# One buffer for each channel tile of the activations, and buffers of its own for folding the norm gains into weights

## The chip, the cores and the metric

The kernel runs on one core of a Trainium2 chip, alone. The metric is the device time of one execution in microseconds. One execution of the kernel was recorded by the hardware profiler; times inside it are counted from its first instruction. PE is the engine of the matmuls, DVE, ACT and POOL are the other compute engines, and SP issues most of the transfers.

## The reference

A trunk of two layers on 2048 positions of 1024 channels, in float32: a gated short convolution, then stick-breaking attention with 8 heads of 64, whose keys and values are projected once.

```python
def _rmsnorm(x, g):
    return x * rsqrt(mean(x * x, axis=-1) + 1e-6) * g

def _short_conv_mixer(h, w_in, w_conv, w_out):
    b_gate, c_gate, xin, g = split(h @ w_in, 4)            # w_in: 1024 x 4096
    y = b_gate * causal_depthwise_conv3(c_gate * xin, w_conv)
    return (y * silu(g)) @ w_out

def _stick_breaking_attention(q, k, v):                    # for each block of 128 queries
    z = q @ k.T * scale
    log_one_minus = where(mask, log_sigmoid(-z), 0)        # mask: strictly causal
    weights = exp(where(mask, z + reverse_cumsum(log_one_minus), -inf))
    return weights @ v

x = x + _short_conv_mixer(_rmsnorm(x, norm_a), w_in_a, conv_a, w_out_a)
k, v = split(_rmsnorm(x, norm_kv) @ w_kv, 2)
q, g = split(_rmsnorm(x, norm_b) @ w_in_b, 2)
x = x + (_stick_breaking_attention(q, k, v) * silu(g)) @ w_out_b
out = _rmsnorm(x, norm_f)
```

## The kernel before

The activations are held transposed, channels on the 128 partitions (eight tiles of 128 channels, k = 0 to 7) and positions along the row, in four chunks c of 512 positions. Every large product is made of three matmuls for each k, on values split into a high and a low part: high weight with high activation, high with low, low with high (`mm3`, line 210). So one product of 128 output channels for one chunk is 24 matmuls of 128x128 by 512 columns. Splitting is a copy on ACT that rounds to the high part and a subtraction that leaves the low part, on DVE or POOL (`split`, line 172).

**Weights.** The first use of a block of weights (1024 x 128) loads it raw (`load_raw`, two buffers `wraw`), splits it into a `whl` tile (`w_tile`, four buffers, 8 KB for each partition) and stores that to memory (`split_w`). Later uses load the stored split (`load_w`). `fold_gains` does the same ahead of time for the 16 blocks of `w_kv` and `w_in_b`: it loads a block raw, multiplies it by the norm's gains on DVE (line 366), splits and stores it. It uses the same two `wraw` and four `whl` buffers as the mixer's weights.

**Activations.** `act_tile` gives a buffer for all eight channel tiles of a chunk, high and low (32 KB for each partition), and there are two of them. In turn they hold h (the normed input), y (the gated convolution, read back), xn (the normed stream after layer 0) and the gated attention output og. A third buffer of 16 KB, `og`, holds x1 (the stream after layer 0, eight tiles) and once og and x2. A buffer is handed to its next tile when everything that reads or writes the old tile is done, transfers included.

**Order of work.** `m01` makes the mixer input products for chunks 0 and 1 together, in eight blocks of columns `cb`. In a block the four weights C, X, B and G are used by chunk 0 and then by chunk 1 (192 matmuls). Beside it run the statistics of chunks 2 and 3 (`stats_x`) and `fold_gains`. Then come the output projection of the mixer and the K, Q, V and gate projections of each chunk, with mixer products of chunks 2 and 3 and the attention of earlier chunks between them. Chunk 3's attention and the last projections end the program. The program is written as such interleaved streams, and a scheduler then fixes the order of the instructions of each engine; each engine and SP's queue run theirs strictly in that order.

Of the kernel before, what the change touches and what calls it, by code (L numbers as in the profile page):

```python
# [14 lines left out]
P = 128  # L15
# [6 lines left out]
NR, NW, NT, NL, NWB, NRAW, NWTS = 5, 8, 4, 5, 4, 2, 2  # L22
# [23 lines left out]
def kernel(  # L46
# [68 lines left out]
    def act_tile(nm):  # L115
        return sb.tile([P, 2, KD, CH], F32R, name=nm, tag="act", bufs=2)
# [59 lines left out]
    def load_raw(src, nm, kt=KD):  # L176
        raw = sb.tile([P, kt, P], F32, name=f"wr_{nm}", tag="wraw", bufs=NRAW)
        if len(src.shape) == 2:
            src = src.rearrange("(k p) n -> p k n", p=P)
        nc.sync.dma_start(out=raw, in_=src)  # L180
        return raw

# [6 lines left out]
    def split_w(raw, key, nm, kt=KD, eng=nc.vector):  # L189

        wt = w_tile(nm, kt)
        split(wt[:, 0], wt[:, 1], raw, eng)
        split_d[key] = dram.tile([P, 2, kt, P], F32, name=f"sw_{nm}")
        nc.sync.dma_start(out=split_d[key], in_=wt.bitcast(F32))
        return wt

    def load_w(src, key, nm, kt=KD, eng=nc.vector):

        if key not in split_d:
            return split_w(load_raw(src, nm, kt), key, nm, kt, eng)  # L200
        wt = w_tile(nm, kt)
        nc.sync.dma_start(out=wt.bitcast(F32), in_=split_d[key])
        return wt
# [6 lines left out]
    def mm3(ps, wts, a, kt=KD):  # L210
# [3 lines left out]
        for k in range(kt):  # L214
            for w, m in ((hi, 0), (hi, 1), (lo, 0)):
                ins = nc.tensor.matmul(ps, w[:, k, :], a[:, m, k, :], start=n == 0, stop=n == 3 * kt - 1)  # L216
# [16 lines left out]
    def norm_x_late(c, between=None):  # L233

        hc = act_tile(f"h_{c}")
        xs = []
        for k in range(KD):
            if k == 1 and between is not None:
# [36 lines left out]
    def norm_x(c):  # L275
        hc = act_tile(f"h_{c}")
        pb = bcast(rx[c], f"hb{c}")
        for k in range(KD):
# [3 lines left out]
            split(hc[:, 0, k, :], hc[:, 1, k, :], x)  # L282
# [78 lines left out]
    def fold_gains():  # L361

        for nm, src, gain in (("kv", w_kv, gains["kv"]), ("b", w_in_b[0], gains["b"])):
            for i in range(KD):
                raw = load_raw(src[:, i * P:(i + 1) * P], f"fold_{nm}{i}")
                nc.vector.tensor_mul(raw, raw, gain.unsqueeze(2).to_broadcast([P, KD, P]))
                split_w(raw, (nm, i), f"{nm}{i}")
# [398 lines left out]
```

## Time and profile before

| | us |
|---|---|
| three runs: median (lowest to highest) | 1909.34 (1906.65 to 1910.77) |
| the profiled execution | 1907.57 |
| its span, first to last instruction | 1905.8 |
| PE busy | 1784.0 (94%) |
| DVE busy | 1264.6 (66%) |
| ACT busy | 769.7 (40%) |
| POOL busy | 436.2 (23%) |
| data moved | 443.64 MB, mean 233 GB/s |

Names in the profile are the program's tile names with buffer numbers left out: `whl_G` is the split weight G of the mixer, `whl_kv` and `whl_b` are folded blocks, `sw_...` is the stored split in memory, `wr_...` is a raw block, `pC`, `pX`, `pB` and `pG` are the mixer products, `po`, `pk`, `pq`, `pv` and `pg` the later projections, and `cs`, `p`, `cv` and `sg` the mixer's intermediate values. L216 is the matmul line of all large products, L173 and L174 are the two halves of every split, and L366 is the fold's multiplication. "SPq" is SP issuing a transfer. A number in brackets with an arrow is the idle time before an instruction and who ended it.

### The profile page before, as it was taken

The page shows a single profiled execution, that of the slowest core. Times are in us where ns is not written, and L with a number is a line of the kernel's source. Part 1 is how long each engine was busy: PE and PEld are TensorE (multiplying, and loading weights), DVE is VectorE, ACT ScalarE, POOL GpSimd, SP SyncE. Part 2 cuts the span into 40 slices and gives each one's busy share as a digit, 9 for nine tenths or more (in the row PEclk, how much of TensorE's full clock was granted, in tenths as well). Part 3 has the DMA queues.
Part 4 walks back from the last instruction along what each step waited for, and adds up shares of the span by engine and source line. Part 5 has one row for each costly group of instructions (what it writes and reads, how often), then busy time and mean ns, then how long its engine had stood idle before and what let it go on. Part 6 is the DMA issues. An engine that isn't in the chain of part 4 may idle for free.

```text
span 1905.8 us, 24702 instructions
## 1 busy us (share of the span) xinstructions
PE 1784.0 (94%) x8312; PEld 1449.4 (76%) x8312; DVE 1264.6 (66%) x1895; ACT 769.7 (40%) x1481; POOL 436.2 (23%) x822
## 2 busy tenths in 40 slices
PE   7899999999999999999999999999979999878785
PEld 5787777778888888888788888888857788656563
DVE  7644554574334264428888346788897999999996
ACT  6312222241123133314545233444555666565553
POOL 5000000000011021103123112222422224654641
PEclk9999999999999999999999999999999999999897
DMA  9648787798887779776767776655746665877751
GB/s 314 210 150 248 248 254 237 243 312 304 295 284 270 258 237 286 246 262 224 242 211 268 238 253 219 202 175 197 258 144 196 197 199 193 284 225 250 252 177 50
DMA packets 226702, 443.64 MB, mean 233 GB/s; under 512 B 16912, under 2 KB 131600, under 8 KB 199952
## 3 DMA queue, kind: packets, MB, share of 16 engines
q1 hardware_dynamic: 166496, 383.30, 60.0%
q10 hardware_dynamic: 59920, 58.74, 10.9%
q8 instruction: 66, 1.08, 0.2%
q14 instruction: 60, 0.49, 0.1%
q0 software_dynamic: 160, 0.02, 0.1%
HBM read 314.34 MB, written 127.66 MB: 232 GB/s over the span
## 4 chain that ended last, share of the span: by engine, by line
PE 69%; DVE 14%; DMA 9%; issue 4%; ACT 2%; POOL 1%; SPq 0%; ACTq 0%; POOLq 0%; DVEq 0%
PE pX L216 8%; PE po L216 7%; PE pG L216 7%; PE pC L216 7%; PE pB L216 6%; PE pg L216 5%; PE pk L216 5%; PE pq L216 5%; PE pv L216 4%; PE wt L512 4%; DVE R L500 4%; PE av L522 3%; DVE w L504 2%; PE av L521 2%; PE z L486 2%
## 5 line engine op out<-in xcount | busy, mean ns | idle before, releaser
L500 DVE TENSOR_TENSOR_SCAN R<-R,R,ones 128x512 f32<-128x512 f32 x192 | 256.6, 1339 | 11.4 <-ACT R L489 11.1
L489 ACT ACTIVATE R<-z 128x512 f32<-128x512 f32 (+1 forms) x320 | 174.2, 544 | 173.1 <-DVE R L500 78.4
L174 DVE TENSOR_TENSOR wtl<-wt,wth 128x512 fp32r<-128x512 f32 (+1 forms) x320 | 185.6, 600 | 67.2 <-ACT wth L173 66.3
L504 DVE TENSOR_TENSOR w<-w,R 128x512 f32<-128x512 f32 (+1 forms) x320 | 212.2, 671 | 21.3 <-POOL R L499 3.0
L173 ACT CAST wth<-wt 128x512 fp32r<-128x512 f32 (+1 forms) x320 | 160.3, 526 | 160.1 <-PE wt L512 137.4
L216 PE MATMUL pC<-h,whl_C 128*128 128x512 f32 x768 | 197.1, 405 | 14.4 <-ACT whl_C L173 8.3
L216 PE MATMUL pG<-h,whl_G 128*128 128x512 f32 x768 | 186.6, 393 | 9.9 <-ACT whl_G L173 9.9
L499 POOL COPY R<-R 128x1 f32<-128x1 f32 x192 | 112.3, 585 | 360.8 <-DVE R L500 293.3
L216 PE MATMUL pX<-h,whl_X 128*128 128x512 f32 x768 | 187.6, 393 | 6.0 <-ACT cs L320 3.9
L216 PE MATMUL po<-y,whl_o 128*128 128x512 f32 x768 | 187.8, 394 | 2.0 <-DVE x L389 1.3
L512 PE MATMUL wt<-ident,w 128*128 128x128 f32 x1088 | 177.8, 278 | 9.2 <-DVE w L504 5.1
L216 PEld LDWEIGHTS pC<-h,whl_C 128*128 128x128 f32 x768 | 148.2, 195 | 49.4 <-ACT whl_C L173 8.3
L216 PE MATMUL pB<-h,whl_B 128*128 128x512 f32 x768 | 185.6, 392 | 0.0
L216 PEld LDWEIGHTS pG<-h,whl_G 128*128 128x128 f32 x768 | 143.2, 188 | 41.0 <-ACT whl_G L173 11.6
L491 ACT ACTIVATE w<-z 128x512 f32<-128x512 f32 (+1 forms) x320 | 172.7, 543 | 0.5 <-PE wt L512 0.5
L216 PEld LDWEIGHTS pX<-h,whl_X 128*128 128x128 f32 x768 | 142.2, 188 | 37.6 <-ACT cs L320 5.1
L216 PEld LDWEIGHTS po<-y,whl_o 128*128 128x128 f32 x768 | 144.2, 189 | 33.5 <-DVE x L389 1.9
L512 PEld LDWEIGHTS wt<-ident,w 128*128 128x128 f32 x1088 | 138.6, 143 | 38.3 <-DVE w L504 7.2
L216 PEld LDWEIGHTS pB<-h,whl_B 128*128 128x128 f32 x768 | 143.0, 188 | 30.1 <-DVE cv L356 0.4
L522 PE MATMUL av<-wtl,vv 128*128 128x512 f32 (+1 forms) x320 | 129.1, 405 | 36.7 <-DVE wtl L174 36.6
L500 DVE TENSOR_TENSOR_SCAN R<-R,ones 128x512 f32<-128x512 f32 (+3 forms) x128 | 116.1, 913 | 33.8 <-POOL R L495 32.2
L486 PE MATMUL z<-kt,q 128*128 128x512 f32 (+1 forms) x320 | 129.1, 405 | 4.1 <-ACT w L491 3.4
(170 smaller groups left out, 2655.3 us busy)
## 6 DMA issues: line engine op xcount, KB each, us to landing
whl_o<-sw_o SPq DMA_DIRECT2D x24, 1024.0 KB, 5.7
kt<-k_d ACTq DMA_DIRECT2D x80, 256.0 KB, 3.6
vv<-v_d ACTq DMA_DIRECT2D x80, 256.0 KB, 4.0
whl_C<-sw_C SPq DMA_DIRECT2D x16, 1024.0 KB, 5.4
whl_X<-sw_X SPq DMA_DIRECT2D x16, 1024.0 KB, 5.5
whl_B<-sw_B SPq DMA_DIRECT2D x16, 1024.0 KB, 5.5
whl_G<-sw_G SPq DMA_DIRECT2D x16, 1024.0 KB, 5.2
whl_k<-sw_kv SPq DMA_DIRECT2D x16, 1024.0 KB, 5.2
```

Of the source, the lines that this page charges most:

```text
L173: nc.scalar.copy(hi, src)
L174: eng.tensor_sub(lo, src, hi.bitcast(F32))
L216: ins = nc.tensor.matmul(ps, w[:, k, :], a[:, m, k, :], start=n == 0, stop=n == 3 * kt - 1)
L486: nc.tensor.matmul(ps[:, lom:CH], q2[:, 0, qi * P:(qi + 1) * P], kt[:, lom:CH], start=True, stop=False)
L489: nc.scalar.activation(R[:, lo + 1:CH + 1], ps[:, lo:CH], AF.Sigmoid, scale=-0.125)
L491: nc.scalar.activation(w[:, lo:CH], ps[:, lo:CH], AF.Sigmoid, scale=0.125)
L499: nc.gpsimd.tensor_copy(R[:, 0:1], carry[qi])
L500: nc.vector.tensor_tensor_scan(out=R[:, lo + 1:CH + 1], data0=R[:, lo + 1:CH + 1], data1=ones[:, 0:1].to_broadcast([P, CH - lo]), initial= ...
L504: nc.vector.tensor_mul(w[:, lo:CH], w[:, lo:CH], R[:, lo:CH])
L512: nc.tensor.transpose(wt[:, qi * P:(qi + 1) * P], ws[qi][:, kb * P:(kb + 1) * P], ident)
L521: nc.tensor.matmul(av[:, 0:n], vs, wh[:, 0:n], start=first, stop=False)
L522: ins = nc.tensor.matmul(av[:, 0:n], vs, wl[:, 0:n], start=False, stop=final)
```

## The change

The two large activation buffers become 16 buffers of one channel tile each (high and low, 4 KB for each partition), taken one by one: `h`, `y`, `xn` and `og` are now lists of eight or four tiles, and a tile's buffer comes free when that tile's own readers are done. The 16 KB buffer `og` becomes eight buffers of 2 KB, which x1 and x2 take one channel tile at a time. og no longer sits in it, but in `act` tiles.

`fold_gains` no longer takes `wraw` and `whl` buffers. It works on half blocks (four of the eight k): two tiles from the eight `og` buffers, one for the high part and one for the low. The raw half block is loaded into the low tile, multiplied there, and split, and each part is stored by a transfer of its own. One folded block was one load of 512 KB and one store of 1024 KB; it is now two loads and four stores of 256 KB each. Nothing is computed differently.

```diff
-NR, NW, NT, NL, NWB, NRAW, NWTS = 5, 8, 4, 5, 4, 2, 2
+NR, NW, NT, NL, NWB, NRAW, NA, NWTS = 5, 8, 4, 5, 4, 2, 16, 2
...
-    def act_tile(nm):
-        return sb.tile([P, 2, KD, CH], F32R, name=nm, tag="act", bufs=2)
+    def act_tile(nm, k):
+        return sb.tile([P, 2, CH], F32R, name=f"{nm}_{k}", tag="act", bufs=NA)
...
             for i in range(KD):
-                raw = load_raw(src[:, i * P:(i + 1) * P], f"fold_{nm}{i}")
-                nc.vector.tensor_mul(raw, raw, gain.unsqueeze(2).to_broadcast([P, KD, P]))
-                split_w(raw, (nm, i), f"{nm}{i}")
+                split_d[nm, i] = dram.tile([P, 2, KD, P], F32, name=f"sw_{nm}{i}")
+                for j in range(0, KD, 4):
+                    hi, lo = (sb.tile([P, 4, P], F32R, name=f"fold{m}_{nm}{i}_{j}", tag="og", bufs=KD) for m in range(2))
+                    raw = lo.bitcast(F32)
+                    nc.sync.dma_start(out=raw, in_=src[j * P:(j + 4) * P, i * P:(i + 1) * P].rearrange("(k p) n -> p k n", p=P))
+                    nc.vector.tensor_mul(raw, raw, gain[:, j:j + 4].unsqueeze(2).to_broadcast([P, 4, P]))
+                    split(hi, lo, raw)
+                    for m, t in enumerate((hi, lo)):
+                        nc.sync.dma_start(out=split_d[nm, i][:, m, j:j + 4, :], in_=t.bitcast(F32))
                 yield 1.0
...
-        y = act_tile(f"y_{c}")
+        y = []
         for k in range(KD):
+            y.append(act_tile(f"y_{c}", k))
             t = ld512(f"yr_{c}_{k}")
             nc.sync.dma_start(out=t, in_=y_d[c][k])
-            split(y[:, 0, k, :], y[:, 1, k, :], t, nc.gpsimd if k in YLP else nc.vector)
+            split(y[k][:, 0, :], y[k][:, 1, :], t, nc.gpsimd if k in YLP else nc.vector)
...
-            if ob == 0:
-                x1 = sb.tile([P, KD, CH], F32, name=f"x1_{c}", tag="og", bufs=1)
-            x = x1[:, ob, :]
+            x = sb.tile([P, CH], F32, name=f"x1_{c}_{ob}", tag="og", bufs=KD)
+            x1.append(x)
...
-        if c not in og_t:
-            og_tile(c)
-        og = og_t[c]
+        og = act_tile(f"og_{c}", k)
+        og_t.setdefault(c, []).append(og)
```

The scheduler then puts the instructions in another order at some places. The first is SP's queue in the mixer stage. Its rows before, around the first folds, which stand behind the weights of the third block of columns (`y_d_2_89` is the store of chunk 0's y of that block):

```order
L194 DMA sw_B_0_1096<-whl_B_0_1093 128x2048
L180 DMA wr_fold_kv_1283<-in_w_kv_dram 128x8x128
L194 DMA sw_G_0_1192<-whl_G_0_1189 128x2048
L180 DMA wr_C_0_1353<-in_w_in_a_dram 128x8x128
L357 DMA y_d_1_96<-cv_1_924 128x512
L357 DMA y_d_2_89<-cv_0_1123 128x512
L377 DMA yr_2_2812<-y_d_2_89 128x512
L194 DMA sw_kv_1289<-whl_kv_1286 128x2048
L180 DMA wr_fold_kv_1387<-in_w_kv_dram 128x8x128
L194 DMA sw_C_0_1358<-whl_C_0_1355 128x2048
```

And now, in that third block, ahead of the same y store; the first fold load stands 63 rows further up, among the loads of the start:

```order
L191 DMA sw_C_0_980<-whl_C_0_975 128x2048
L188 DMA wr_B_0_1106<-in_w_in_a_dram 128x8x128
L367 DMA sw_kv_1727<-fold_kv_4_1737 128x512
L363 DMA fold_kv_4_1828<-in_w_kv_dram 128x4x128
L367 DMA sw_kv_1818<-fold_kv_0_1819 128x512
L367 DMA sw_kv_1818<-fold_kv_0_1820 128x512
L191 DMA sw_X_0_1073<-whl_X_0_1068 128x2048
L188 DMA wr_G_0_1202<-in_w_in_a_dram 128x8x128
L363 DMA fold_kv_0_1933<-in_w_kv_dram 128x4x128
L367 DMA sw_kv_1818<-fold_kv_4_1827 128x512
```

The folds have moved ahead: 13 of the 32 half blocks have been asked for at the end of these rows, where before one block of 16 was ahead of that y store, and the last store of a folded half stands before the y of the fifth block. From the y store of chunk 0's second block to that of its third, SP has nine fold loads, 18 fold stores, four raw weights, four spills of split weights and three y transfers. The eight loads of x1 for chunk 0, which stood at the start ahead of raw G, now stand behind the folds.

The second place is ACT at the end of the mixer stage, where the first y is split. Before (`y_2803` is the one tile of chunk 0's y):

```order
L173 CAST whl_G_0_2639<-wr_G_0_2637 128x1024
L173 CAST y_2803<-yr_0_2804 128x512
L173 CAST y_2803<-yr_1_2808 128x512
L173 CAST y_2803<-yr_2_2812 128x512
L173 CAST y_2803<-yr_3_2816 128x512
L320 COPY cs_1_2701<-pC_1_2676 128x512
L173 CAST whl_b_2736<-wr_fold_b_2733 128x1024
L173 CAST y_2803<-yr_4_2820 128x512
L351 ACTIVATE sg_0_2669<-sg_0_2669 128x512
```

And now:

```order
L334 ACTIVATE cv_0_2764<-p_0_2727,cw 128x512
L174 CAST y_0_2961<-yr_0_2962 128x512
L174 CAST y_1_2966<-yr_1_2967 128x512
L174 CAST y_2_2971<-yr_2_2972 128x512
L174 CAST y_3_2976<-yr_3_2977 128x512
L174 CAST y_4_2981<-yr_4_2982 128x512
L174 CAST y_5_2986<-yr_5_2987 128x512
L174 CAST y_6_2991<-yr_6_2992 128x512
L345 ACTIVATE sg_0_2818<-sg_0_2818 128x512
L314 COPY cs_1_2850<-pC_1_2825 128x512
```

Seven splits of y stand in a row ahead of `sg` and `cs`, each on a tile of its own, and no folded block stands between. On PE, the G product of chunk 0, which before was broken up after two matmuls in four of the eight blocks with the other chunk's C product put between, is now whole in these four.

The third place is DVE in the first block, between the inverse norms of chunk 0 and their use. Before:

```order
L155 TENSOR_SCALAR dg_h_1_422<-ident,yl_h_417 128x128 x4
L170 TENSOR_TENSOR acc_h_995<-acc_h_995,sq_h_1001 128x512
L174 TENSOR_TENSOR whl_G_0_442<-wr_G_0_440,whl_G_0_442 128x1024
L333 TENSOR_TENSOR p_0_377<-p_0_377,rs_0_430 128x512
L341 SCALAR_TENSOR_TENSOR cv_0_435<-p_0_377,cw,cv_0_435 128x512
```

And now:

```order
L156 TENSOR_SCALAR dg_h_1_429<-ident,yl_h_419 128x128 x4
L171 TENSOR_TENSOR acc_h_1009<-acc_h_1009,sq_h_1015 128x512
L175 TENSOR_TENSOR whl_G_0_447<-wr_G_0_448,whl_G_0_447 128x1024
L175 TENSOR_TENSOR whl_C_0_709<-wr_C_0_710,whl_C_0_709 128x1024
L364 TENSOR_TENSOR fold_kv_4_1307<-fold_kv_4_1307,g_kv 128x512
L171 TENSOR_TENSOR acc_h_1009<-acc_h_1009,sq_h_1020 128x512
L327 TENSOR_TENSOR p_0_384<-p_0_384,rs_0_437 128x512
```

A split of C and a fold's multiplication stand ahead of `p` here, and the two operations of the first fold stand further up; the third fold follows before the norms of chunk 1 are used. Between the first multiplication by chunk 1's norms and the multiplication of its convolution by B stood three sums of squares of this kind (`acc_h`), and now stands one.

More of the change, by code (lines that the diff above doesn't have):

```diff
@@ L174, in split @@
         eng.tensor_sub(lo, src, hi.bitcast(F32))
[L176 to L181, printed above, removed]
     def w_tile(nm, kt=KD):
@@ L187 @@
     split_d = {}
[L189 to L195, printed above, removed]
     def load_w(src, key, nm, kt=KD, eng=nc.vector):
         if key not in split_d:
-            return split_w(load_raw(src, nm, kt), key, nm, kt, eng)
+            wt = w_tile(nm, kt)
+            raw = sb.tile([P, kt, P], F32, name=f"wr_{nm}", tag="wraw", bufs=NRAW)
+            nc.sync.dma_start(out=raw, in_=src.rearrange("(k p) n -> p k n", p=P))
+            split(wt[:, 0], wt[:, 1], raw, eng)
+            split_d[key] = dram.tile([P, 2, kt, P], F32, name=f"sw_{nm}")
+            nc.sync.dma_start(out=split_d[key], in_=wt.bitcast(F32))
+            return wt
         wt = w_tile(nm, kt)
@@ L215, in mm3 @@
             for w, m in ((hi, 0), (hi, 1), (lo, 0)):
-                ins = nc.tensor.matmul(ps, w[:, k, :], a[:, m, k, :], start=n == 0, stop=n == 3 * kt - 1)
+                ins = nc.tensor.matmul(ps, w[:, k, :], a[k][:, m, :], start=n == 0, stop=n == 3 * kt - 1)
                 if fine[1] and len(anchors) > SLACK and n % GRP == 0:
@@ L281, in norm_x @@
                                            op0=ALU.mult, op1=ALU.mult)
-            split(hc[:, 0, k, :], hc[:, 1, k, :], x)
+            hc.append(act_tile(f"h_{c}", k))
+            split(hc[k][:, 0, :], hc[k][:, 1, :], x)
         return hc
@@ L392, in proj_out @@
             yield rest(24)
-        xn = act_tile(f"xn_{c}")
+        kept[c] = []
         pb = rstd_bcast(acc, f"x1{c}")
         for k in range(KD):
-            t = x1[:, k, :]
-            nc.vector.tensor_mul(t, t, pb)
-            split(xn[:, 0, k, :], xn[:, 1, k, :], t, nc.gpsimd if k in XNL else nc.vector)
-        kept[c] = xn
+            xn = act_tile(f"xn_{c}", k)
+            nc.vector.tensor_mul(x1[k], x1[k], pb)
+            split(xn[:, 0, :], xn[:, 1, :], x1[k], nc.gpsimd if k in XNL else nc.vector)
+            kept[c].append(xn)
         yield YP[c] * 24 * MM
@@ L568, in gated @@
             nc.gpsimd.tensor_mul(r, r, sg)
-        split(og[:, 0, k, :], og[:, 1, k, :], r)
+        split(og[:, 0, :], og[:, 1, :], r)
     def gated_in(c, ks=range(4)):
@@ L621, in out_b_last @@
     def out_b_last(c):
-        og, x2 = og_t[c], x2_t[0]
+        og = og_t[c]
+        x2 = [sb.tile([P, CH], F32, name=f"x2_{c}_{k}", tag="og", bufs=KD) for k in range(KD)]
         for ob in range(KD):
@@ L628, in out_b_last @@
             yield from mm3(ps, wts, og, kt=3)
-            nc.sync.dma_start(out=x2[:, ob, :], in_=x1_d[c][ob])
-            nc.vector.tensor_add(x2[:, ob, :], x2[:, ob, :], ps)
+            nc.sync.dma_start(out=x2[ob], in_=x1_d[c][ob])
+            nc.vector.tensor_add(x2[ob], x2[ob], ps)
             yield rest(9)
@@ L658, in out_b_last @@
             if k in (1, 4, 7):
[L659 to L660 removed]
+                nc.scalar.activation(x2[k], x2[k], AF.Copy, scale=gains["f"][:, k:k + 1])
+                nc.gpsimd.tensor_mul(x2[k], x2[k], pbs)
             else:
[L662 removed]
+                nc.vector.scalar_tensor_tensor(out=x2[k], in0=x2[k], scalar=gains["f"][:, k:k + 1],
                                                in1=pb, op0=ALU.mult, op1=ALU.mult)
[L664 removed]
+            nc.sync.dma_start(out=outT[k * P:(k + 1) * P, cols(c)], in_=x2[k])
         yield 0.0
```

35 lines of the change are left out of this document (11 added, 24 removed).

## The prediction

> **What bounds the kernel now.** I read the page first, then the stretches of the whole span, then PE's waits inside the stretch that has room, then the timeline around one such wait.
>
> ```profile
> span 1905.8 us, 24702 instructions
> PE 1784.0 (94%) x8312; PEld 1449.4 (76%) x8312; DVE 1264.6 (66%) x1895; ACT 769.7 (40%) x1481; POOL 436.2 (23%) x822
> PE 69%; DVE 14%; DMA 9%; issue 4%; ACT 2%; POOL 1%; SPq 0%; ACTq 0%; POOLq 0%; DVEq 0%
> ```
>
> PE works 1784.0 of 1905.8 us, and the chain that ended last runs on PE for 69%. So a change pays only where PE stands still (121.8 us) or runs at a lower clock. Where that is, the stretches say (after the times: busy time and instruction count of PE, its weight loads, DVE, ACT, POOL; then granted clock, DMA share, GB/s):
>
> ```profile
> 0.00:100.00 100.00, 83.38 (x343) 65.17 (x344) 66.17 (x125) 45.78 (x72) 28.78 (x34) 0.97 0.79 253
> 100.00:400.00 300.00, 284.12 (x1231) 231.68 (x1231) 154.23 (x190) 71.68 (x88) 13.96 (x28) 0.99 0.75 233
> 400.00:1400.00 1000.00, 995.85 (x4762) 827.35 (x4761) 587.94 (x918) 359.76 (x745) 183.28 (x449) 1.00 0.75 249
> 1400.00:1460.00 60.00, 45.36 (x204) 32.89 (x204) 57.07 (x99) 35.60 (x72) 16.69 (x36) 0.94 0.38 124
> 1460.00:1600.00 140.00, 137.01 (x713) 113.20 (x713) 123.40 (x165) 84.72 (x172) 39.83 (x81) 1.00 0.64 205
> 1600.00:1906.00 306.00, 238.32 (x1068) 179.10 (x1066) 275.79 (x402) 172.12 (x336) 153.69 (x194) 0.90 0.64 206
> ```
>
> PE idles 16.6 us before 100, 15.9 us from 100 to 400, 4.2 us in the thousand microseconds after, 14.6 us from 1400 to 1460 and 67.7 us from 1600 on. In the last two DVE is full (57.07 of 60, 275.79 of 306), and the change takes no DVE work from them. From 400 to 1400 nothing can be won. The stretch from 100 to 400, in which the norm gains are folded into `w_kv` and `w_in_b`, is the change's own, and DVE is half empty there. PE's waits from 90 to 440:
>
> ```profile
> PE pG L216 <- ACT whl_G L173: 9.9, 4, 2.8
> PE pX L216 <- ACT cs L320: 3.9, 3, 2.5
> PE pX L216 <- DVE cv L356: 2.1, 2, 1.5
> ```
>
> Four waits for the G weights are 9.9 us, and 6.0 us come with them on pX. One of the four in order of time:
>
> ```profile
> 168.55 0.45 SPq L180 DMA_DIRECT2D wr_G<-in_w_in_a_dram  x1
> 174.51 0.32 SPq L194 DMA_DIRECT2D sw_kv<-whl_kv  x1
> 179.62 1.04 ACT L173 CAST whl_G<-wr_G 128x1024 fp32r<-128x1024 f32 x1 [3.05 <-DMA sw_kv<-whl_kv]
> 180.72 1.22 PE L216 MATMUL pG<-h,whl_G 128*128 128x512 f32 x2 [2.76 <-ACT whl_G L173]
> 181.74 6.50 PE L216 MATMUL pC<-h,whl_C 128*128 128x512 f32 x23
> 321.82 5.40 PE L216 MATMUL pC<-h,whl_C 128*128 128x512 f32 x23
> ```
>
> The raw G weights were asked for at 168.55 (median to landing 7.3 us by the list of DMA issues below, so about 175.9), yet ACT splits them only at 179.62, when the store of a folded tile (`sw_kv`, issued 174.51) has landed. That tile sat in one of the four `whl` buffers. Without it ACT could begin at about 175.9, 3.7 us sooner, more than the 2.76 us that PE waits. After this wait 23 matmuls take 6.50 us; the same 23 at 321.82 take 5.40. So a wait can cost a low clock as well.
>
> **The change part by part.** *The fold leaves `whl` and `wraw`.* The four waits on G go: 9.9 us. Of the 6.0 us on pX, the largest is this one, with what blocked ACT:
>
> ```profile
> 368.94 6.79 PE L216 MATMUL pC<-h,whl_C 128*128 128x512 f32 x23
> 380.75 2.18 ACT L173 CAST y<-yr 128x512 fp32r<-128x512 f32 x4 [12.66 <-PE pG L216]
> 383.47 5.76 PE L216 MATMUL pX<-h,whl_X 128*128 128x512 f32 x24 [2.52 <-ACT cs L320]
> ```
>
> ACT stood 12.66 us at the first split of y, because the whole y tile takes the buffer of h, which the last pG reads to its end; `cs`, for which pX waits, is queued behind it. *With a buffer for each channel tile* y_0 follows the third of that pG's 24 matmuls and y_6 the 21st, so seven of the eight tiles are split while pG still runs, and `cs` comes behind pC as it must. The 2.52 us go. The two 0.68 us waits behind a late pG and the 1.53 us behind a late B split (the rest of 3.9 and the larger part of 2.1) go with the shared buffers. The last 0.6 us (2.1 - 1.5) stay: at 123 us DVE stood at a fold's multiply for its load while `cv` waited behind. Such standing is 15.8 us for the 16 folds of today,
>
> ```profile
> L366 DVE TENSOR_TENSOR wr_fold_kv<-wr_fold_kv,g_kv 128x1024 f32<-128x1024 f32 x8 | 9.8, 1222 | 8.6 <-DMA wr_fold_kv<-in_w_kv_dram 8.6
> L366 DVE TENSOR_TENSOR wr_fold_b<-wr_fold_b,g_b 128x1024 f32<-128x1024 f32 x8 | 9.8, 1222 | 7.2 <-DMA wr_fold_b<-in_w_in_b_dram 7.2
> ```
>
> and costs PE 0.6; with 32 loads I take twice that, 1.2 us. The low clock behind two of the four waits (6.50 and 6.79 against 5.40) is 1.1 + 1.4 = 2.5 us and goes with them. Sum: 9.9 + 6.0 + 2.5 = 18.4 us to win, 1.2 back.
>
> The Trainium skill (TensorE: Matmul & The Clock Gate, What's actually happening) says the clock falls after an idle window of about 3.4 us. Here waits of 2.76 and 2.10 us were followed by slow matmuls, so the measurement decides; by the rule the 2.5 us would not hang on these waits, and the sum would be 15.9.
>
> *The halves.* Each fold becomes two: 32 multiplies and 32 subtractions of 512 columns on DVE and 32 copies on ACT in place of 16 each of 1024. A 128x512 operation on DVE and ACT is this:
>
> ```profile
> L333 DVE TENSOR_TENSOR p<-p,rs 128x512 f32<-128x512 f32 x13 | 9.0, 692 | 0.4
> L173 ACT CAST y<-yr 128x512 fp32r<-128x512 f32 x7 | 3.9, 615 | 12.7 <-PE pG L216 12.7
> L174 DVE TENSOR_TENSOR whl_kv<-wr_fold_kv,whl_kv 128x1024 fp32r<-128x1024 f32 x8 | 9.8, 1222 | 12.5 <-ACT whl_kv L173 12.5
> L173 ACT CAST whl_kv<-wr_fold_kv 128x1024 fp32r<-128x1024 f32 x8 | 8.4, 1053 | 23.0 <-DVE wr_fold_kv L366 16.8 <-PE pC L216 6.3
> ```
>
> DVE pays 64 x 0.692 - 32 x 1.222 = 5.2 us more and ACT 32 x 0.615 - 16 x 1.053 = 2.8 us. Both lie in a stretch where DVE is busy 154 of 300 us and ACT 72, beside PE. Without that cover it would be the 5.2 us.
>
> *The fold moves ahead.* Today the last folded tile is stored at 386 us; in SP's new order the first fold load stands among the loads of the start, and all folds are out before the y of the fifth of the eight blocks of mixer columns.
>
> ```profile
> 385.65 0.32 SPq L194 DMA_DIRECT2D sw_b<-whl_b  x1
> ```
>
> Between the first-chunk y stores of blocks two and three stand nine fold loads and 18 fold stores (256 KB each), four weight loads (512 KB), four spills (1024 KB) and three y transfers: 14.2 MB for one block of 192 matmuls, 43.5 us (192 x 5.44 / 24, by the row of pB below), or 325 GB/s. Against it:
>
> ```profile
> 80.00:100.00 20.00, 20.00 (x91) 16.57 (x90) 6.34 (x9) 1.40 (x3) 0.55 (x3) 1.00 0.04 14
> 233.00:280.00 47.00, 45.47 (x201) 37.35 (x200) 24.21 (x28) 10.94 (x13) 1.60 (x4) 1.00 0.87 268
> 410.00:420.00 10.00, 10.00 (x46) 8.29 (x45) 8.55 (x14) 4.82 (x8) 0.00 (x0) 1.00 1.04 377
> ```
>
> The engines stand idle from 80 to 100 today. At full share they move 268 / 0.87 = 308 GB/s in the fold's stretch and 377 later, so a block needs 38 to 46 us: just about its own length. SP falls behind by at most 2.5 us a block, 8 us over the 28 folds (3.1 blocks) that matter. What that may cost is the lead of the weights:
>
> ```profile
> 103.14 0.43 SPq L180 DMA_DIRECT2D wr_B<-in_w_in_a_dram  x1
> 128.90 5.44 PE pB L216 x24
> wr_G<-in_w_in_a_dram SPq DMA_DIRECT2D x8, 512.0 KB, 7.3
> wr_fold_kv<-in_w_kv_dram SPq DMA_DIRECT2D x8, 512.0 KB, 6.4
> y_d<-cv SPq DMA_DIRECT2D x32, 256.0 KB, 4.5
> whl_o<-sw_o SPq DMA_DIRECT2D x24, 1024.0 KB, 5.7
> ```
>
> Where no fold stands between, raw B is asked for 25.8 us before its first matmul; 7 to 8.5 us for landing and 2.3 for the split leave about 15. So 8 us of lag are covered. SP is one queue, though: a fold's store waits there for ACT and DVE, and a fold's load for a buffer. Eight buffers hold four folds. One fold's round is its load (4.5, the 256 KB row, to 6.4, twice the size), three steps on DVE and ACT (2.0) with hand-overs and turns in the queues (1 to 5), and its stores (4.5 to 8): 12 to 21 us. Nine a block need no more than 4 x 43.5 / 9 = 19.3 us. I take 16, in the middle, and from there no stall; at the upper end, 21, the lag is 28 x 21 / 4 - 135 = 12 us, still within 15. For small stalls in this stretch I take 2 us, between none and 5.
>
> The Trainium skill (DMA: Bandwidth & Descriptors, Rules for kernel authors) speaks against the halves: at least 1 MiB for each DMA. Its measured table has 6.15 us for 1 MB and 0.95 for 64 KB; an estimate from it is 2.0 us for 256 KB, so four take 1.9 us more than one, 8 us a block, 33 us of lag and some 18 us of stalls, which would make the gain nothing. In the trace a 256 KB y store lands in 4.5 us beside 5.7 for 1024 KB, in traffic, which does not settle what it takes of the engines.
>
> *The front.* Until 70 us DVE is the crowded engine, and three folds (six operations, 4.1 us) now stand among the chain that frees the buffer for this matmul:
>
> ```profile
> 70.24 7.92 PE L216 MATMUL pC<-h,whl_C 128*128 128x512 f32 x24 [4.26 <-DVE cv L345]
> 64.90 0.69 DVE L333 TENSOR_TENSOR p<-p,rs 128x512 f32<-128x512 f32 x1 [1.57 <-ACT rs L261]
> ```
>
> Against that, the eight 256 KB loads of x1 that stood before the G weights have gone behind, DVE had 1.57 us to spare here, and two of the three sums of squares between `p` and `cv` are moved behind it (1.4 us at 0.69). Bounds +4 and -2; I take +0.5.
>
> *The rest.* x1, xn, og and x2 in single tiles come free sooner, but from 400 to 1400 PE is full, and from 1400 DVE is, with the same work: 0, with 4 us either way for another order of attention and projections.
>
> Total: -18.4 + 1.2 + 2 + 0.5 = -14.7, taken as -14.5 against the profiled execution's 1907.57 (1.8 around its span). The runs' median is 1.8 above it: 1909.3 - 14.5 = 1894.8.
>
> **The rivals.** *Slower: the folds hold up SP.* If a fold's round takes 26 us, 28 of them take 182 us where 135 were meant; 47 us of lag less the 15 us of lead are 32 us of PE waits for raw weights, against 17 won: 1924. It decides from a round of 24 us on. For it: SP does stand for DVE's splits today,
>
> ```profile
> SPq L194 <- DVE whl_kv L174: 42.7, 8, 13.5
> ```
>
> up to 13.5 us for one. Against: a round of 24 us needs every part of it at its worst at once. 11%.
>
> *No change: small transfers are dear.* A block at 250 GB/s takes 57 us; 13 x 3.1 = 41, less 15, gives 26 us; at 275 GB/s it is 51.5 us, and 25 - 15 = 10 us stay; around 262 the gain is gone: 1909. Against it are the 308 and 377 above. This is also where the skill's rule leads. 10%.
>
> *Half the gain.* X and B weights had little to spare too, and a stall that no longer happens at G happens one weight later; or the front loses its 4 us and the y splits still hold `cs`: 1907.6 - 8 + 1.8 = 1901. 17%.
>
> **How the numbers follow.** The forecast (1889 to 1899) has 62%, half the gain 17%, no change 10%, slower 11%. Faster by over 0.2% (3.8 us, about what a measurement of this kernel can tell from none) takes the first two: 0.79; same 0.10; slower 0.11. The time is that of the likeliest case, 1894.8. The range of 8 in 10 runs from 1887 (all 18.4, and 4 us by luck of order) to 1909, where the gain is gone.
>
> **What would show it.** Right: in the first 400 us no wait of pG for `whl_G`, no 12 us wait of ACT at the first y, the folds over by about 205 to 235 us, DMA share near 1 from 100 to 200, PE's idle time from 100 to 400 down from 15.9 to about 4 us, and the first po some 14 us sooner, a lead that stays to the end. Wrong: waits of pB, pX or pC for raw weights between 140 and 230 (SP held up), a longer wait at pC near 70 us (the front), or the lead lost after 1400, where DVE sets the end.

## The result, and the profile after

The changed kernel takes 1899.46 us (median of 7 runs, 1893.57 to 1902.85) against 1909.34 us before (7 runs, not three as the table ahead has it, 1906.65 to 1910.77): a ratio of 0.9947, 95% interval 0.9931 to 0.9963. Predicted were 1894.8 us in a range of 1887 to 1909. The time won is 9.9 us where 14.5 were forecast, so the sign and the stretch were right and about a third of the amount is missing. The profiled execution took 1899.87 us, 7.7 less than the one before it was set against.

The page of the changed kernel, and then its stretches (columns as in the prediction: busy time and count of PE, PEld, DVE, ACT, POOL; granted clock, DMA share, GB/s):

```profile
span 1898.2 us, 24937 instructions
PE 1787.5 (94%) x8312; PEld 1453.6 (77%) x8312; DVE 1264.4 (67%) x1927; ACT 771.9 (41%) x1497; POOL 433.3 (23%) x822
```

```profile
0.00:100.00 100.00, 84.30 (x350) 66.31 (x351) 75.97 (x143) 52.50 (x82) 32.06 (x34) 0.97 0.93 297
100.00:400.00 300.00, 294.15 (x1288) 242.40 (x1287) 159.68 (x231) 76.29 (x105) 14.55 (x28) 0.99 0.75 244
400.00:1400.00 1000.00, 990.04 (x4745) 821.14 (x4745) 586.91 (x918) 361.66 (x752) 182.98 (x457) 1.00 0.73 243
1400.00:1460.00 60.00, 52.73 (x225) 39.36 (x225) 49.02 (x82) 29.73 (x61) 13.31 (x30) 0.90 0.54 171
1460.00:1600.00 140.00, 132.28 (x671) 107.53 (x670) 126.07 (x165) 85.73 (x176) 46.41 (x92) 0.99 0.61 192
```

From 100 to 400 us PE now stands idle for 5.9 us instead of 15.9, and the DMA engines, which had pauses in the first 100 us (share 0.79), are at 0.93 there. PE's waits from 90 to 440 us are one row:

```profile
PE pX L208 <- DVE cv L350: 5.9, 3, 3.2
```

No wait for a G weight is left, and none on `cs`. What the change won up to there can be read at the first output projection. These two rows, before and after, list the po matmuls in a short window; the two times in us are the starts of the first and of the last:

```profile
L216 PE MATMUL po<-y,whl_o x8: 389/389/389, 400.2 to 401.8; 128*128 128x512 f32 x8
```

```profile
L208 PE MATMUL po<-y,whl_o x12: 389/389/389, 385.5 to 388.0; 128*128 128x512 f32 x12
```

The lead is 14.7 us at the first po and still 14.2 us at the last one (it started at 1396.7 us, now at 1382.5). Behind that, half of it is lost. The stretch from the start of the last po to the end, as one window, before and after:

```profile
1396.70:1905.80 509.10, 423.98 (x2000) 327.86 (x1998) 459.56 (x670) 294.55 (x584) 211.58 (x315) 0.93 0.61 196
```

```profile
1382.50:1898.20 515.70, 432.42 (x2000) 333.43 (x1998) 459.17 (x670) 293.02 (x584) 208.57 (x313) 0.92 0.60 194
```

In both VectorE works through 670 instructions, all but two or three of them the same, and is busy for 459.6 and 459.2 us, but the stretch is 509.1 us long before and 515.7 after. VectorE stands idle for 49.5 us in the one and 56.5 in the other. That is the 7 us, and it is a loss in idle time, not in work.

### The profile page after: what moved, and what is told of

Its sections match the earlier page's. It is cut to its first block, busy times and chain, and to the rows that moved or that the text cites. A ratio compares the mean times of both kernels' runs of the same rounds, so it can differ in the third digit from the quotient of the medians.

```text
span 1898.2 us, 24937 instructions
## 1 busy us (share of the span) xinstructions
PE 1787.5 (94%) x8312; PEld 1453.6 (77%) x8312; DVE 1264.4 (67%) x1927; ACT 771.9 (41%) x1497; POOL 433.3 (23%) x822
## 4 chain that ended last, share of the span: by engine, by line
PE 68%; DVE 17%; DMA 6%; issue 5%; ACT 2%; POOL 1%; SPq 0%; ACTq 0%; POOLq 0%; DVEq 0%
PE pX L208 8%; PE pB L208 7%; PE po L208 7%; PE pC L208 7%; PE pG L208 7%; DVE R L501 5%; PE pv L208 4%; PE pk L208 4%; PE wt L513 4%; PE pq L208 4%; PE pg L208 4%; DVE w L505 3%; PE av L523 3%; DVE wtl L175 2%; PE av L522 2%
## 5 line engine op out<-in xcount | busy, mean ns | idle before, releaser
L208 PE MATMUL pC<-h,whl_C 128*128 128x512 f32 x768 | 193.3, 401 | 14.4 <-ACT whl_C L174 8.2
L500 POOL COPY R<-R 128x1 f32<-128x1 f32 x192 | 103.9, 541 | 349.3 <-DVE R L501 302.2
L501 DVE TENSOR_TENSOR_SCAN R<-R,ones 128x512 f32<-128x512 f32 (+3 forms) x128 | 116.8, 918 | 36.0 <-POOL R L496 32.5
```

The costliest lines, as they stand in the source:

```text
L208: ins = nc.tensor.matmul(ps, w[:, k, :], a[k][:, m, :], start=n == 0, stop=n == 3 * kt - 1)
L500: nc.gpsimd.tensor_copy(R[:, 0:1], carry[qi])
L501: nc.vector.tensor_tensor_scan(out=R[:, lo + 1:CH + 1], data0=R[:, lo + 1:CH + 1], data1=ones[:, 0:1].to_broadcast([P, CH - lo]), initial= ...
```

## The experiments

### Which half of the change wins

`fold_alone` is the kernel before with the new fold only. Its halves go through slices of the 16 KB in which x1 stands later:

```
+        ring = sb.tile([P, 8, 4, P], F32R, name="fold_ring", tag="og", bufs=1)
...
+                for j in range(0, KD, 4):
+                    hi, lo = (ring[:, 2 * (nf[0] % 4) + m] for m in range(2))
```

> Only the fold part of the change, on the kernel before: the halves go through slices of one 16 KB tile that stands where x1 stands later; activations and gates stay whole tiles as before. Theory FOLD (nearly the whole lead of 14.7 us at the first po comes from the fold's own buffers, the finer activations give the 2.5 us of the first y): first po at 386 to 390 us, no wait for a G weight between 140 and 230 us, time 1895 to 1902 us. Rival ACT (the finer activations carry the gain, the fold alone only moves its waits): first po at 395 us or later, time 1904 us or more.

Measured: 1898.06 us, ratio 0.9941 (0.9924 to 0.9958), first po at 388.6 us. `acts_alone` is the other half: the changed kernel with the old fold.

```
+                raw = sb.tile([P, KD, P], F32, name=f"wr_fold_{nm}{i}", tag="wraw", bufs=NRAW)
...
+                wt = w_tile(f"{nm}{i}")
+                split(wt[:, 0], wt[:, 1], raw)
```

> Only the activation part, on the kernel after: one buffer for each channel tile of activations, gates and x1, while the fold goes through the raw and split weight buffers as before. Theory FOLD: the four G waits of about 2.5 us stay, only the first y starts some 2.5 us sooner; first po at 396 to 400 us, time 1905 to 1911 us. Rival ACT: first po at 390 us or sooner, time 1901 us or less. A third reading, TAIL: if the finer activations by themselves lose time after 1400 us, this run is slower than the kernel before, 1911 to 1916 us.

Measured: 1916.82 us, ratio 1.0043 (1.0028 to 1.0058), first po at 399.0 us. PE's waits, of the fold alone (from 90 to 400 us, then from 0 to 90) and of the activations alone (90 to 400 us):

```profile
PE pX L216 <- DVE cv L356: 3.1, 3, 1.9
```

```profile
PE pC L216 <- DVE cv L345: 9.6, 1, 9.6
```

```profile
PE pG L208 <- ACT whl_G L174: 9.9, 4, 3.2
PE pX L208 <- ACT cs L314: 3.0, 3, 1.6
PE pX L208 <- DVE cv L350: 1.8, 2, 1.2
```

With the activations alone the four G waits stand as they stood, 9.9 us. With the fold alone they are gone. The first half of theory FOLD holds: the fold's own buffers win the stretch, and in time the fold alone gains as much as both halves together (0.9941 beside 0.9947). The second half does not: by themselves the finer activations move the first po by 1.2 us and not by 2.5. ACT stands less at the first y, but the last y splits wait for their loads ahead of `cs`, and pX still waits 1.62 us:

```profile
381.36 0.62 ACT L174 CAST y<-yr 128x512 fp32r<-128x512 f32 x1 [0.79 <-DMA yr<-y_d]
```

```profile
382.52 5.75 PE L208 MATMUL pX<-h,whl_X 128*128 128x512 f32 x24 [1.62 <-ACT cs L314]
```

The fold alone also shows what the front could have cost. Its pC near 70 us waits 9.6 us, because in that order VectorE runs seven fold operations between `p` (65.94 us) and the multiply that frees pC's buffer (75.84 us). In the changed kernel none stands there, and the same wait is 3.11 us, less than the 4.26 before:

```profile
68.98 3.35 PE L208 MATMUL pC<-h,whl_C 128*128 128x512 f32 x7 [3.11 <-DVE cv L339]
```

Behind the last po the activations alone lose time: 516.3 us to the end where before had 509.1, as a row says; the fold alone takes 512.5 there.

```profile
1400.10:1916.40 516.30, 429.57 (x2000) 329.60 (x1998) 461.32 (x670) 292.98 (x584) 207.87 (x313) 0.93 0.61 194
```

That, with 4.6 us more between the first and the last po (1001.1 us, 996.5 before), and not the front, makes them slower than the kernel before. The third reading, TAIL, comes nearest, though it had only the end and at most 1916 us.

### Is the loss behind the last po luck, or one buffer?

`after_again` is the changed kernel once more.

> The changed kernel once more, for a second profile of it. Theory ORDER (the 7 us of lead that it loses between 1380 and 1600 us come from the order of its instructions and stand in every execution): the same waits of VectorE at vt and khl near 1456 and 1464 us, 5 to 7 us each, and a lead at the last pg 6 to 8 us smaller than at the last po; times 1897 to 1902 us. Rival LUCK (the loss hangs on when the transfers land in one execution): those waits differ by more than 3 us in all and the time goes with them, down to 1893 us where they are short.

Measured: 1897.33 us, ratio 0.9940 (0.9924 to 0.9955); its profiled execution took 1894.97. The first po is at 382.2 us, 3.3 sooner than in the first profile, and the last po at 1377.3; from there to the end it is 516.0 us, within 0.3 us of the first profile. So these two executions differ by 3.3 us ahead of the first po and by 1.9 between the first and the last, and the stretch behind the last po is as long in both. VectorE again waits there, 6.3 us at vt and 7.1 at khl, where ORDER had 5 to 7 at each.

In the first profile of the changed kernel VectorE waits there, from 1383 to 1599 us, above all for two splits, of vt and of khl. ACT began that of vt only when the store of q had landed (the row below the list); k, q and v splits share one buffer (tag `hl`):

```profile
DVE vt L175 <- ACT vt L174: 6.5, 1, 6.5
DVE khl L175 <- ACT khl L174: 5.7, 1, 5.7
DVE wtl L175 <- ACT wth L174: 3.9, 6, 1.5
```

```profile
1455.58 0.59 ACT L174 CAST vt<-pvt 128x512 fp32r<-128x512 f32 x1 [6.56 <-DMA q_d<-qhl]
```

Before, the waits at the splits that share this buffer were shorter (1397 to 1604 us):

```profile
DVE wtl L174 <- ACT wth L173: 6.7, 5, 4.0
DVE khl L174 <- ACT khl L173: 3.7, 1, 3.7
DVE qhl L174 <- ACT qhl L173: 2.4, 1, 2.4
```

`after_vt` gives the v split other buffers, which lie free there:

```
-        vt = sb.tile([P, 4, 2, 2, 64], F32R, name=f"vt_{c}_{vb}", tag="hl", bufs=1)
+        vt = sb.tile([P, 4, 2, 2, 64], F32R, name=f"vt_{c}_{vb}", tag="wraw", bufs=NRAW)
```

> The changed kernel with the split transposed v blocks (vt) in the two raw-weight buffers, which lie free from 400 us on but for the output weights, instead of the one buffer that they share with khl and qhl. Theory HL (the lead is lost because vt and khl wait for the q store that holds that one buffer): the VectorE waits of 6.5 us at vt and 5.7 us at khl shrink below 2 us in all, the lead at the last pg stays at 12 us or more, time 1892 to 1896 us. Rival ORDER/CLOCK (the loss lies in the low clock and in the stretch of few matmuls from 1383 to 1426 us, and the hl waits are covered): time 1898 to 1902 us as the changed kernel.

Measured: 1896.55 us, ratio 0.9936 (0.9919 to 0.9952). VectorE's waits from 1383 to 1598 us:

```profile
DVE wtl L175 <- ACT wth L174: 5.4, 8, 1.9
DVE R L501 <- ACT R L490: 5.4, 6, 1.7
DVE R L501 <- POOL R L496: 2.9, 1, 2.9
DVE khl L175 <- ACT khl L174: 2.7, 2, 2.3
```

The waits at vt and khl fall from 12.2 to 2.7 us, but the stretch from the last po to the end falls only from 516 to 514.4: the idle time turns up at other instructions. The one buffer is where VectorE stands, not why the stretch is longer. Theory HL, which wanted the lead kept and 1892 to 1896 us, falls; the 1.6 us by which the stretch is shorter are less than two executions of one kernel can differ by there (4.6 us, below).

### Is it the loads that moved?

With single tiles, x2 (the sum that `out_b_last` finishes) can be loaded as soon as x1's tiles come free. Its eight loads were issued at 1655 us before and are issued at 1420 us now; SP's rows, before and after:

```profile
1655.02 0.91 SPq L629 DMA_DIRECT2D x<-x_d  x2
1656.92 2.84 SPq L629 DMA_DIRECT2D x<-x_d  x4
1661.71 0.94 SPq L629 DMA_DIRECT2D x<-x_d  x2
```

```profile
1420.34 10.42 SPq L616 DMA_DIRECT2D x<-x_d  x8
```

`after_x2late` puts the gates of chunk 0 into x1's buffers again, so that x2 comes late:

```
+        if c == 0:
+            og = Pair(sb.tile([P, CH], F32R, name=f"og{m}_{c}_{k}", tag="og", bufs=KD) for m in range(2))
+        else:
             og = act_tile(f"og_{c}", k)
```

> The changed kernel, but the gates of chunk 0 stand in the eight 2 KB buffers of x1 again, as they stood in x1's buffer before; so the eight loads of x2 (256 KB each, out_b_last), which in the changed kernel run at 1420 to 1431 us, go back to about 1650 us. Seen so far from the last po to the end: 509.1 us before, 515.7 and 516.0 in two profiles of the changed kernel, 516.3 with the finer activations alone, 512.5 with the fold alone; the x2 loads run early in just the three with some 516. Theory X2 (the early loads, 2 MB in the crowded stretch, make the one hl buffer's stores land late): that stretch falls to 509 to 512.5 us, the q store lands within 4 us instead of 7, time 1892 to 1895 us. Rival ORDER (another order of VectorE's work costs it, the loads are beside the point): 515 us or more, time 1897 to 1900 us.

Measured: 1902.56 us, ratio 0.9961 (0.9947 to 0.9975). The loads are back at 1648 to 1658 us, the waits at vt, khl and qhl are down from 13.4 to 4.7 us, and the stretch is longer still:

```profile
1383.30:1902.00 518.70, 432.17 (x2000) 333.06 (x1998) 461.68 (x669) 293.19 (x584) 217.31 (x313) 0.92 0.60 193
```

Theory X2 falls too. It had fitted the profiles up to then; the kernel made for it spoke against it.

### Does VectorE's standing at fold multiplies cost the 5.9 us?

One of the three waits at pX, in order of time, on VectorE and then on PE:

```profile
120.41 0.69 DVE L364 TENSOR_TENSOR fold_kv<-fold_kv,g_kv 128x512 f32<-128x512 f32 x1 [3.06 <-DMA fold_kv<-in_w_kv_dram]
...
124.07 0.69 DVE L350 TENSOR_TENSOR cv<-cv,pG 128x512 f32<-128x512 f32 x1
```

```profile
124.90 7.34 PE L208 MATMUL pX<-h,whl_X 128*128 128x512 f32 x24 [3.20 <-DVE cv L350]
```

VectorE stands 3.06 us at a fold's multiply until its load has landed; behind it waits the multiply that frees PE's buffer. Ahead of the other two waits at pX it stands 2.44 and 1.97 us at such a multiply. `after_foldpool` takes the fold off VectorE and ScalarE:

```
-                    nc.vector.tensor_mul(raw, raw, gain[:, j:j + 4].unsqueeze(2).to_broadcast([P, 4, P]))
-                    split(hi, lo, raw)
+                    nc.gpsimd.tensor_mul(raw, raw, gain[:, j:j + 4].unsqueeze(2).to_broadcast([P, 4, P]))
+                    nc.gpsimd.tensor_copy(hi, raw)
+                    nc.gpsimd.tensor_sub(lo, raw, hi.bitcast(F32))
...
-                nc.gpsimd.tensor_copy(p[:, CH:CH + 2], halo[:, cb, :])
+                nc.scalar.copy(p[:, CH:CH + 2], halo[:, cb, :])
```

> The changed kernel with the fold's arithmetic (multiply, high half, subtraction) all on GpSimd, and the two small halo copies of each mixer block on ScalarE instead, so that no fold instruction stands on VectorE or ScalarE. Theory STAND (the 5.9 us that TensorE waits at pX for the last multiply of cv come from VectorE standing at fold multiplies for their loads): those waits fall below 1.5 us, the first po comes at 379 to 382 us instead of 385.5, the end 3 to 6 us sooner, time 1893 to 1896 us. Rival DMA (the loads are late for everything in this stretch and the wait only moves, to a weight's split or to the first y): first po at 384 us or later, time 1898 us or more.

Measured: 1895.99 us, ratio 0.9927 (0.9912 to 0.9942), first po at 382.9 us. PE's waits, from 90 to 400 us and then in the first 90:

```profile
PE pX L208 <- DVE cv L350: 0.5, 1, 0.5
```

```profile
PE prb_h L157 <- DVE dg_h L156: 4.3, 1, 4.3
```

The 5.9 us are 0.5: STAND holds for these waits. The edit takes the fold's own work off VectorE as well, so the part of the standing alone is not measured by itself. The first po came a little later than STAND said (379 to 382), for the front lost 4.7 us (pG of the second block of columns at 92.7 us, 88.0 in the changed kernel): PE waited 4.3 us for the broadcast of the first chunk's norm, 1.3 us in the changed kernel. VectorE makes that norm, and beside the folds on GpSimd some of its operations took longer. The first of these rows is of `after_foldpool`, the second of the changed kernel; why the same four operations take 2.23 us there was not tested.

```profile
42.20 2.23 DVE L156 TENSOR_SCALAR dg_h<-ident,yh_h 128x128 fp32r<-128x128 f32 x4
```

```profile
40.62 0.87 DVE L156 TENSOR_SCALAR dg_h<-ident,yh_h 128x128 fp32r<-128x128 f32 x4
```

`after_both` joins this edit and the late x2.

> Both edits of the two runs above together. If X2 and STAND both hold and add: first po at 379 to 382 us, 509 to 512.5 us from the last po to the end, time 1887 to 1891 us. If only one of them holds: 1892 to 1896 us. If neither: 1897 to 1900 us.

Measured: 1892.50 us (1890.12 to 1894.87), ratio 0.9908 (0.9893 to 0.9923): the best of all. First po at 384.0 us, and behind the last po

```profile
1379.50:1888.40 508.90, 427.54 (x2015) 333.69 (x2013) 459.14 (x671) 296.00 (x587) 206.01 (x316) 0.93 0.61 197
```

Its last stretch is 508.9 us, with `after_foldpool` at 514.8. The late x2 thus goes with 5.9 us less here and, in `after_x2late`, with about 3 us more. The two edits do not add as the expectation had it (1887 to 1891 us); a buffer's place as such does not explain the stretch.

### What smaller transfers cost

`after_128k` cuts each of the fold's transfers in two:

```
+                    for q in (0, 2):
+                        nc.sync.dma_start(out=raw[:, q:q + 2], in_=src[(j + q) * P:(j + q + 2) * P, i * P:(i + 1) * P].rearrange("(k p) n -> p k n", p=P))
```

> The changed kernel with each of the fold's transfers cut in two: loads and stores of 128 KB instead of 256 KB, 192 instead of 96 of them, the same bytes, buffers and arithmetic. Theory WIDE (the fold's pace is set by the bytes and the eight buffers; smaller transfers cost next to nothing): the DMA share and rate of the first 100 us stay within 5% (0.93, 297 GB/s), fold over within 5 us of the changed kernel, time 1897 to 1902 us. Rival SMALL (each transfer has a cost of its own that grows as they get smaller; by the rate of 250 GB/s of the prediction's rival): rate in the first 100 us at 275 GB/s or lower, TensorE waits for the fold or the weights return between 100 and 250 us, time 1903 us or more.

Measured: 1904.21 us, ratio 0.9962 (0.9948 to 0.9976), first po at 389.2 us. PE's one wait from 90 to 400 us, and two stretches, of `after_128k` and then of the changed kernel:

```profile
PE pX L208 <- DVE cv L350: 7.8, 3, 2.9
```

```profile
0.00:100.00 100.00, 84.01 (x339) 65.41 (x340) 75.45 (x141) 51.20 (x79) 30.27 (x34) 0.97 0.95 289
100.00:250.00 150.00, 142.24 (x622) 116.47 (x620) 86.61 (x130) 40.88 (x58) 6.04 (x13) 0.99 0.90 291
```

```profile
100.00:250.00 150.00, 144.15 (x627) 118.21 (x626) 87.32 (x131) 39.83 (x57) 6.54 (x13) 0.99 0.88 298
```

Neither theory has it whole. The rate falls by 2 to 3%, from 297 to 289 and from 298 to 291 GB/s, as WIDE allowed; but the last fold stores go out at 235 us instead of 224, VectorE stands longer at the fold's loads, and the time is over 1903 us as SMALL said. At 256 KB no cost shows in the first 100 us: by rate and share the engines moved 297 / 0.93 = 319 GB/s for a full share, and 253 / 0.79 = 320 before. At 128 KB it is 289 / 0.95 = 304, so there the size of a transfer begins to cost. Whether the later stores come from that or from SP, which issues 192 transfers in place of 96, is not shown.

### Order, tested by itself

Ten profiles by now had a last stretch from 508.9 to 518.7 us with VectorE busy 459 to 463 us in all. In the three that share one order of instructions from the last po on (the changed kernel, `after_again`, `after_128k`; the sequence in the traces is the same on every engine, with 668 instructions on VectorE) it was 515.7, 516.0 and 516.8 us, with leads of 14.2, 19.4 and 11.0 us at its start. So the next runs test the order: one changes nothing, two change one number that sets the order and nothing that is computed, and the last moves one piece of the front to another engine.

> The kernel before once more, for a second profile. Theory ORDER (the length of the stretch from the last po to the end belongs to the order of the instructions there and to nothing else): 508 to 510.5 us again. Rival LUCK: it lies as far off 509.1 as the changed kernel's 516, in either direction.

Measured: 1909.88 us, ratio 1.0002 (0.9990 to 1.0015). The profiled execution, 1915.15 us, is a long one, and its last stretch, in the same order as before, is 513.7 us:

```profile
1399.80:1913.50 513.70, 429.05 (x2000) 334.25 (x1998) 460.51 (x670) 295.33 (x584) 214.41 (x315) 0.92 0.61 194
```

ORDER's 508 to 510.5 is missed: one order varies by 4.6 us between two executions. That is two thirds of the loss, so a pair of profiles cannot settle what the loss is due to.

`before_f0` is the kernel before with one share changed, far ahead of the stretch:

```
-F0, F1, F2, F3, F4 = 0.4, 0.5, 0.65, 0.4, 0.6
+F0, F1, F2, F3, F4 = 0.45, 0.5, 0.65, 0.4, 0.6
```

> The kernel before with one share changed, F0 from 0.4 to 0.45: it says how much of the third mixer's emission goes beside the first chunk's projections, at about 400 to 560 us. Nothing in the program of the last 500 us is touched, its buffers neither, but the scheduler then gives VectorE another order there. Theory ORDER: the stretch from the last po to the end is not 509 us any more but somewhere among those seen with other orders, 511 to 519 us, and the time is 1911 us or more, if the first po stays within 3 us of 400. Rival BUFFERS (the 509 us of before belong to its whole tiles, the 516 us to one buffer for each channel tile): 508 to 510.5 us.

Measured: 1920.07 us, ratio 1.0059 (1.0042 to 1.0077). The first po is at 400.6 us (402.1 in `before_again`), the last po at 1400.1 (1399.8), and then

```profile
1400.10:1918.70 518.60, 431.98 (x2000) 334.76 (x1998) 462.44 (x669) 294.15 (x584) 214.15 (x313) 0.92 0.60 193
```

The program and the buffers of this stretch are those of the kernel before; only the order is another, on VectorE and in the traces on the other engines and on SP too. It takes 518.6 us, 9.5 and 4.9 more than the two executions of before, and VectorE is idle for 56.2 us of it, as in the changed kernel. This does not hang on one profile: its four runs took 1917.04 to 1920.50 us, and the 23 of the kernel before that were taken beside them 1904.23 to 1912.67 (`before_again`: to 1915.15). ORDER holds here: order alone can make the whole of the loss.

`after_yn` is the changed kernel with another order:

```
-YN = 2.0
+YN = 2.5
```

> The changed kernel with one cost changed, YN from 2.0 to 2.5, which holds back the emission of the third and fourth mixers after their norm; the last 500 us are untouched but for VectorE's order there. Theory ORDER: the stretch from the last po to the end is at least 2 us off the 515.7 to 516.8 us that the changed order has had in three profiles, likelier below than above (510 to 514 us). Rival BUFFERS: 515 to 517.5 us.

Measured: 1910.41 us, ratio 1.0016 (1.0003 to 1.0029). Its last stretch is 512.6 us, 3.1 to 4.2 less than the changed order's, as ORDER said, though that is within the 4.6 us that one order can vary by; and the new order has its own stall elsewhere, this pC, and the first pk comes 13.6 us later than in the changed kernel. The lead of 14 us at the first po is all but gone before 500 us.

```profile
463.29 8.61 PE L208 MATMUL pC<-h,whl_C 128*128 128x512 f32 x24 [9.70 <-DVE cv L339]
```

`both_sq0` is `after_both` with the second chunk's sums of squares on VectorE.

```
-            square_into(acc, x, k == 0, f"h{c}{k}", nc.gpsimd, early=True)
+            square_into(acc, x, k == 0, f"h{c}{k}", nc.vector if c else nc.gpsimd, early=True)
```

> The version with the fold on GpSimd and x2 in its late place, and beside it the sums of squares of the second chunk's norm on VectorE instead of GpSimd, where three of them stood between fold instructions. Theory QUEUE (that is why the first pG of this version came at 48.4 us instead of 41.9 and TensorE waited 4.3 us for the norm's broadcast): the 4.3 us fall below 2 us, the first po comes at 379 to 382 us instead of 384.0, and with a last stretch between 508 and 516 us the time is 1887 to 1894 us. Rival (VectorE at the front is as full as GpSimd and the norm comes as late): first po at 383 us or later, time 1892 to 1897 us.

Measured: 1894.86 us, ratio 0.9923 (0.9906 to 0.9940). The wait of 4.3 us for the broadcast is gone (1.4 us in two waits), the first pG is at 41.0 us and not 48.4, and the first po at 382.4, just outside QUEUE's 379 to 382. But QUEUE's reason does not hold. The norm comes no sooner, as its rival had it; PE's new order puts the first matmuls of pG ahead of the broadcast (`prb_h`), so that PE has work meanwhile. The first row is of `after_both`, the other two of `both_sq0`:

```profile
45.68 0.77 PE L157 MATMUL prb_h<-dg_h,onesr 128*128 128x512 f32 x1 [4.32 <-DVE dg_h L156]
```

```profile
40.96 0.61 PE L208 MATMUL pG<-h,whl_G 128*128 128x512 f32 x2
...
45.50 0.40 PE L157 MATMUL prb_h<-dg_h,onesr 128*128 128x512 f32 x1
```

But the last stretch is 515.4 us where `after_both` had 508.9, in yet another order, and the kernel is no faster.

## Why the prediction was right, and where it was not

Its sum, term by term, in us, against the two profiles of before and after:

| term | predicted | measured |
|---|---|---|
| the four waits for G weights | -9.9 | -9.9 |
| waits at pX: 6.0 won, 1.2 and 2 given back | -2.8 | -0.1 (6.0 to 5.9) |
| low clock behind waits | -2.5 | -2.7 |
| front, up to pG of the second block | +0.5 | -0.9 (88.9 to 88.0) |
| rest up to the first po (what is left of the sum) | 0 | -1.1 |
| first po | -14.7 | -14.7 (400.2 to 385.5) |
| first po to last po | 0 | +0.5 |
| last po to the end | 0, with 4 either way | +6.6 (509.1 to 515.7) |

That the first po came at -14.7 to the tenth is luck: the waits at pX fell 2.7 us short of their term, and the front, the rest and the clock made it up. By the second executions of the two kernels (402.1 and 382.2 us) the lead there is 19.9 us.

**The fold's buffers.** Right, mechanism and size: the G waits go with the fold's own buffers and stay without them (`fold_alone`, `acts_alone`). The low clock went along: between pG of the second block and the first po, 43 of about 1280 matmuls started 0.235 to 0.6 us behind the one before (longer distances are the waits), 4.7 us over the usual 0.227 in all; after the change it is 20 and 2.0 us. In the second executions it is 51 with 6.2 us and 8 with 0.4.

**Standing at the fold's multiplies.** Right that it stays, wrong in size. It was taken as 0.6 us doubled to 1.2, with 2 us for small stalls beside it; it is 5.9 us. The standing itself did double, from 15.8 to 32.5 us, but its price did not stay at 0.6 us for 15.8: with the DMA engines at 0.91 of their time from 100 to 200 us, three loads land late just where the multiply that frees PE's buffer stands behind them. `after_foldpool` has 0.5 us with the fold off VectorE. In a second execution of the changed kernel it was 4.6.

**The front.** Bounds of +4 and -2 were given and -0.9 came. `fold_alone` shows that the danger was real: 9.6 us of waiting at that pC, 6.5 us lost by pG of the second block.

**The halves.** Right: from 0 to 250 us the engines moved 297 and 298 GB/s, below the 308 taken for a full share and well above the 262 at which the small-transfer rival had the gain gone, the last fold store was issued at 223.6 us (205 to 235 was said), and no wait of pB, pX or pC for raw weights came up between 140 and 230, so SP was not held up by enough to matter. The rival of dear transfers is not wrong in kind: at half the size again the first po is 3.7 to 7.0 us later than in the two profiles of the changed kernel. The rule of at least 1 MiB for each DMA (the Trainium skill, DMA: Bandwidth & Descriptors, Rules for kernel authors), from which the prediction estimated that the gain would be nothing, was not borne out at 256 KB: PE got its lead, and in the first 100 us the rate for a full share was 319 GB/s beside 320 before.

**Half the gain.** The time, 1899.46 us, is just outside the likeliest case (1889 to 1899) and nearer to this rival's 1901 than to 1894.8. But none of its reasons came: no stall moved from G to a raw weight of X or B, the front did not lose 4 us, and `cs` is not held up.

**The step that failed** is the rest: "from 1400 DVE is [full], with the same work: 0, with 4 us either way". The term named another order as what could move it and held that to 4 us. The work is the same (459.56 and 459.17 us), but the engine is not full: in the profiles it stands idle for 50 to 57 us of that stretch, and how much hangs in part on the order in which the scheduler puts the instructions. The prediction's own rows from 1400 us on had 456 of 506 us busy. The sign of being wrong that it named last, the lead lost after 1400, came for half of the lead. The change gave the stretch another order, and the lead "that stays to the end" shrank by 6.6 us in the pair of profiles; by the means of the two profiles of before (511.4) and the three with the changed order (516.2) by 4.8. `before_f0` shows that order alone can do this much in an unchanged program; that it is what did it in the changed kernel is likely and not shown, and which part of the order does it is not settled: the shared buffer of k, q and v and the early loads of x2 were tried, and undoing neither brought the stretch back.

## What to carry to other kernels

Price a change up to the point where another engine takes over, and for the stretch behind it do not write zero because the work is the same: look at how much idle time that engine has there, for a reordering can give or take a good part of it. When a scheduler sets the order, a change in one buffer reorders the program hundreds of microseconds away, so compare profiles stretch by stretch and time more than one version before a loss is put down to the edit itself. Work that waits for transfers belongs on an engine behind which nothing urgent stands.

## What the runs showed of the hardware

The clock fell behind a wait of 3.20 us: 24 matmuls at 124.90 us took 7.34 us, with a mean granted clock of 0.77, where 24 behind a wait of 1.62 us in the same profile took

```profile
171.93 5.69 PE L208 MATMUL pX<-h,whl_X 128*128 128x512 f32 x24 [1.62 <-DVE cv L350]
```

with a granted clock of 1.00. In the second execution of the same kernel that wait was 1.76 us, and the 24 matmuls took 5.72 us. So 1.4 us of wait cost 1.6 us of slow matmuls on top, and most of the 3.3 us by which the two executions differ at the first po comes from this one place. The Trainium skill (TensorE: Matmul & The Clock Gate, What's actually happening) puts the idle window at about 3.4 us; here 3.20 us was enough, as 2.76 and 2.10 us were before. Nor does the length of a wait decide it alone: behind 1.93 us the 24 matmuls were slow in `after_vt`, and behind 2.95 us they were not in `after_128k`.

```profile
171.55 7.32 PE L208 MATMUL pX<-h,whl_X 128*128 128x512 f32 x24 [1.93 <-DVE cv L350]
```

```profile
193.88 5.73 PE L208 MATMUL pX<-h,whl_X 128*128 128x512 f32 x24 [2.95 <-DVE cv L350]
```
